# Gate and up projections by one level of Strassen's algorithm, in two passes over the weights

## The chip, the cores and the metric

The kernel runs on one core of one Trainium2 chip. Its time is the device time of one execution in microseconds (us); of before there are three runs. Times inside an execution are read from one profiled execution by the hardware profiler. TensorE (PE) multiplies matrices, VectorE (DVE), ScalarE (ACT) and GpSimd (POOL) work on vectors, and SyncE (SP) issues the DMA transfers, in the order of its own queue.

## The reference

One layer of a conditioned hybrid decoder, on a sequence of 2048 rows with a model width of 1024 and a feed-forward width of 2816:

```python
h   = _modulate(x, ln1_g[l], sh1, sc1)         # RMSNorm, scale and shift
u   = h @ w_in[l]                              # queries, keys, values of both head groups
...                                            # fox attention (8 heads x 64), differential attention (4 x 128)
x = x + g1[:, None, :] * (mixed @ w_out[l])
h2 = _modulate(x, ln2_g[l], sh2, sc2)
y = (jax.nn.silu(h2 @ w_gate[l]) * (h2 @ w_up[l])) @ w_down[l]
x = x + g2[:, None, :] * y
```

Inputs and output are f32. The change touches the last four lines.

## The kernel before

**Precision.** Every large product is made from 16-bit floats. An f32 operand is scaled by a power of two, cast to fp16 (the high part, on ScalarE, `cast_scaled`, L139) and the rest is cast again (the low part, on VectorE, `sub_scaled`, L144). A product is then three matmuls: high x high, high x low, low x high. The scale comes from a bound: the largest absolute value of each row (`absmax`, VectorE, L123), then the largest of the column of 128 (`colmax`): by GpSimd's all-reduce over partitions (L104), or, if a bank's tag is given, by a matmul that transposes the column into a bank of PSUM (L108) and a VectorE maximum (L109). `pow2` (L115 to L119) makes the scale in four small VectorE operations.

**Stages.** The attention of eight head groups runs first, and ends near 1600 us. The out projection (`out_proj`) makes the new `x` in 16 blocks of 128 rows; a block's row statistics follow at once. All 16 blocks of the new `x` stay on chip (`x1s`), in tiles of four. `norm2` normalises a block, splits it into high and low, and transposes it by a DMA (L953) into `h2s`. Blocks 0 to 7 are done beside attention and out projection, blocks 8 to 15 inside the first chunk below.

**Feed-forward.** 2816 columns are 22 tiles of 128. The loop at the end of `trunk` runs over 11 chunks `c` of two tiles, and in each over four groups `tck` of 512 rows. For a group, `gate_up` makes four results of 128x512 (two tiles, gate and up), each by 8 x 3 matmuls (L1036) in a bank of tags `st` or `pv`; `swiglu` joins gate and up (L1042 on ScalarE, L1043 on VectorE). One step later the joined tile is bounded (`act_row`), split (`act_split`) and multiplied by the down weight: `down` has 16 blocks of 128x512 a chunk and four rows each, six matmuls to a block (L1068), and VectorE adds each bank onto the rows of `x1s` (L1070). So the down products of a group lie between the gate/up products of the next one. Each weight is loaded once: `gu_load` (L981), `gu_row`, `gu_scale`, `gu_split` for gate and up, `dn_load` (L1006; VectorE's bound L1007, GpSimd's product with the gate row L1008), `dn_row`, `dn_scale`, `dn_split` for down. `weight_steps` says at which of 16 steps of a chunk the next chunk's weights are treated.

**What sets the order.** The code is written in the order of these loops; the framework then reorders the instructions of each engine by its own model of their times (`schedule_with_timeline_sim=True`). The order on an engine is fixed in the program, and an instruction that waits holds back those behind it on its engine. Buffers come from pools: `stage()` has three buffers of 128x1024 f32, the large tiles `htile()` and `mtile()` four each of 128x4096 f32, and PSUM has banks of the tags `ip` (1), `st` (2), `pv` (2) and `mx` (3).

## Time and profile before

| | us |
|---|---|
| median of 3 runs | 3000.74 |
| the runs | 2998.21 to 3001.41 |
| the profiled execution | 3000.15 |
| its span in the trace | 2998.4 |
| TensorE busy, of the span | 2819.1 |
| VectorE busy | 1816.3 |
| ScalarE busy | 1199.1 |
| GpSimd busy | 1016.1 |

The profiled execution's time is 1.75 us above its span. The mean granted clock of TensorE over the span is 0.986 of full speed. In a row of the trace, L1036 is line 1036 of the kernel, `out<-in` are the tiles that an instruction writes and reads, and what stands in brackets is the idle time of the engine just before, and what ended it. Matmuls overlap one another, so their single durations (some 0.38 us) add up to more than the time they take together; what one costs is the length of a stretch over their number.

### The profile page before, as it was taken

To read this page: it belongs to the slowest core of one execution; us is meant where nothing else is said; L and a number is where in the kernel's file an instruction comes from. 1 tells how busy PE (TensorE), PEld (TensorE's weight loads), DVE (VectorE), ACT (ScalarE), POOL (GpSimd) and SP (SyncE) were. 2 spreads that over 40 slices of the span, in tenths; PEclk is the share of its full clock that TensorE was granted. 3 is DMA by queue.
4 is the path that set the end of the run, shared out by engine and by line. 5 is a ranking of instruction groups with operands and counts; after the bars stand their busy time and mean duration, and the time that the engine had idled before them with its cause. 6 is when DMAs were issued, how large, how long until landed. Compare 5 with 4: busy or idle time off the path is not lost.

```text
span 2998.4 us, 49306 instructions
## 1 busy us (share of the span) xinstructions
PE 2819.1 (94%) x19346; PEld 1524.8 (51%) x19346; DVE 1816.3 (61%) x3883; ACT 1199.1 (40%) x2323; POOL 1016.1 (34%) x1073
## 2 busy tenths in 40 slices
...
GB/s 225 78 77 59 61 75 38 81 48 65 71 53 90 51 96 101 61 124 107 131 104 105 93 27 29 21 22 35 22 29 22 29 28 22 29 22 31 12 22 91
DMA packets 227530, 186.40 MB, mean 62 GB/s; under 512 B 176984, under 2 KB 193752, under 8 KB 227040
## 3 DMA queue, kind: packets, MB, share of 16 engines
...
q14 instruction: 83, 0.68, 0.1%
...
## 4 chain that ended last, share of the span: by engine, by line
PE 52%; DVE 4%; DMA 3%; ACT 2%; POOL 1%; issue 1%; SPq 0%; POOLq 0%; ACTq 0%; DVEq 0%
PE ps_mx L1068 14%; PE ps_pv L1036 14%; PE ps_st L1036 14%; PE ps_ip L929 3%; PE ps_ip L437 2%; DMA wide<-wide 1%; PE ps_mx L546 1%; PE ps_st L579 1%; PE ps_st L580 1%; DVE stg L952 0%; PE ps_pv L609 0%; POOL pxs L593 0%; DMA stg<-in_w_down_dram 0%; DMA mt<-stg 0%; ACT pxs L585 0%
## 5 line engine op out<-in xcount | busy, mean ns | idle before, releaser
L593 POOL TENSOR_TENSOR pxs<-pxs 128x512 f16<-128x512 f32 (+3 forms) x640 | 693.6, 1099 | 383.7 <-ACT pxs L590 214.2
L437 PE MATMUL ps_ip<-wbuf,ht 128*128 128x384 f16 (+1 forms) x2952 | 569.4, 335 | 20.4 <-DVE vts L144 9.1
L1068 PE MATMUL ps_mx<-dnb,wide 128*128 128x512 f16 x2112 | 485.5, 380 | 13.4 <-DVE ht L1070 10.5
L585 ACT ACTIVATE pxs<-ps_st,cells 128x512 f32<-128x512 f32 (+3 forms) x640 | 390.7, 620 | 251.5 <-PE ps_st L580 117.0
L437 PEld LDWEIGHTS <-ht 128*128 128x128 f16 x3072 | 298.8, 100 | 259.8 <-issue 69.8
L1036 PEld LDWEIGHTS <-mt 128*128 128x128 f16 x2688 | 263.0, 98 | 320.4 <-ACT mt L139 3.5
L104 POOL PARTITION_ALL_REDUCE t_cm<-t_am x84 | 32.7, 398 | 1060.4 <-DVE t_am L123 1037.2
L1070 DVE SCALAR_TENSOR_TENSOR ht<-ps_mx,t_ai,ht 128x512 f32<-128x512 f32 x264 | 196.6, 747 | 302.5 <-PE ps_mx L1068 302.5
L590 ACT ACTIVATE pxs<-pxs 128x512 f16<-128x512 f32 (+3 forms) x640 | 351.2, 565 | 10.5
L607 PE MATMUL ps_pv<-vts,pxs 128*128 128x129 f16 (+1 forms) x2176 | 341.6, 206 | 5.2 <-DVE os L626 5.0
L608 PE MATMUL ps_pv<-vts,pxs 128*128 128x128 f16 (+1 forms) x2176 | 343.8, 208 | 0.0
L609 PE MATMUL ps_pv<-vts,pxs 128*128 128x129 f16 (+1 forms) x2176 | 326.5, 206 | 18.0 <-POOL pxs L593 17.4
L1068 PEld LDWEIGHTS <-wide 128*128 128x128 f16 x2112 | 206.6, 98 | 264.1 <-issue 11.9
L548 DVE TENSOR_REDUCE t_mxc<-ps_mx 128x1 f32<-128x512 f32 x384 | 256.1, 681 | 68.3 <-PE ps_mx L546 67.3
L139 ACT ACTIVATE wide<-wide,t_as 128x1024 f16<-128x1024 f32 x44 | 50.5, 1148 | 597.5 <-DVE t_as L116 597.5
L1036 PEld LDWEIGHTS <-gub 128*128 128x128 f16 x1536 | 150.7, 98 | 185.0 <-issue 3.2
L546 PE MATMUL ps_mx<-mt 71*128 71x512 f16 (+7 forms) x640 | 198.9, 350 | 47.6 <-DVE t_mxc L548 37.7
L609 PEld LDWEIGHTS <-pxs 128*128 128x128 f16 x2176 | 206.7, 98 | 64.0 <-POOL pxs L593 32.4
L607 PEld LDWEIGHTS <-pxs 128*128 128x128 f16 x2176 | 207.5, 97 | 54.1 <-ACT pxs L585 3.5
L1042 ACT ACTIVATE wide<-ps_st,t_gi 128x512 f32<-128x512 f32 x88 | 60.2, 684 | 432.1 <-PE ps_st L1036 432.0
L579 PE MATMUL ps_st<-mt 67*128 67x512 f16 (+7 forms) x640 | 223.7, 350 | 6.6 <-ACT pxs L585 6.3
L608 PEld LDWEIGHTS <-pxs 128*128 128x128 f16 x2176 | 207.4, 97 | 37.7 <-issue 7.3
...
## 6 DMA issues: line engine op xcount, KB each, us to landing
...
```

Of the source, the lines that this page charges most:

```text
L437: T.matmul(pt[:, 0:N], lhsT=h4[:, k, hs, c : c + P], rhs=w4[k // 4][:, k % 4, ws, 0:N], start=(i == 0), stop=(i == len(terms) - 1))
L546: T.matmul(b[:, 0:w], lhsT=QA[0:K, qb * P : (qb + 1) * P], rhs=K2[0:K, c0 : c0 + w], start=True, stop=True)
L548: V.tensor_reduce(out=mx[:, 4 * j + n : 4 * j + n + 1], in_=b[:, 0:w], op=ALU.max, axis=AX.X)
L579: T.matmul(b[:, c0:QC], lhsT=K2[0:K, kb * P : (kb + 1) * P], rhs=QA[0:K, q0:q1], start=True, stop=False, skip_group_check=True)
L585: A.activation(p32[:, c0:QC], b[:, c0:QC], AF.Exp, bias=pshift, scale=1.0)
L590: A.activation(ph[:, c0:QC], p32[:, c0:QC], AF.Copy, bias=0.0, scale=1.0)
L593: (V if hilo[1] == "V" else G).tensor_tensor(out=pl[:, c0:QC], in0=p32[:, c0:QC], in1=ph[:, c0:QC], op=ALU.subtract)
L607: T.matmul(pv[:, jj, :], lhsT=lhs_h, rhs=v4[:, kb, h, 0 : W + 1], start=first, stop=False, skip_group_check=True)
L608: T.matmul(pv[:, jj, 0:W], lhsT=lhs_h, rhs=v4[:, kb, h, W + 2 : 2 * W + 2], start=False, stop=False, skip_group_check=True)
L609: T.matmul(pv[:, jj, :], lhsT=lhs_l, rhs=v4[:, kb, h, 0 : W + 1], start=False, stop=end, skip_group_check=True)
L1036: T.matmul(b.rearrange("p (b n) -> p b n", b=4), lhsT=e["g"][:, w, k, ws, :], rhs=h4[:, :, 2 * k + hs, :], start=(k == 0 and z == 0), stop ...
L1068: T.matmul(b, lhsT=aT[:, as_, f, j * P : (j + 1) * P], rhs=dn[f][:, ws, n * 512 : (n + 1) * 512], start=(f == 0 and z == 0), stop=(f == CH ...
```

## The change

Gate and up are computed by one level of Strassen's algorithm. A pair of tiles (256 columns), a sum over 1024 and a half of the rows are each cut in two, so that a result of four quarters of 128x512 takes seven products of half the depth in place of eight. There are now two passes over the rows (the even and odd blocks of 1024 rows are the two halves of a product's columns), each over all 11 pairs of tiles; a step `q` of the new loop is one pair in one pass, 22 in all, and `w` is 0 for gate and 1 for up. Gate, up and down weights are loaded and split in each pass, so twice.

- Each product (`product`) has 4 x 3 matmuls, and the products run in the order 4, 5, 1, 2, 3, 7, 6. Products 2 and 3 are added onto the banks of 4 and 5, after ScalarE has copied these. The other sums of the quarters are made by VectorE from PSUM and by GpSimd between tiles on chip; then Silu and the product of gate and up.
- Five sums of the weights are made by GpSimd (`gu_sum`) from a raw tile of 128x2048, of which there is one (`raw`); the host packs gate and up weights so that a load is 1 MB. The bound is taken over 2048 columns, with a factor of two.
- Seven sums of the normalised rows are needed (`norm_sum`): two blocks are normalised (`norm_row`), added or subtracted on GpSimd, split, and transposed by a DMA. For the first half they go to four tiles on chip (`comb`) beside attention and out projection; for the second half they are made in the steps q = 2, 4, 6, 8, stored to DRAM (`hcd`), and loaded onto the first half's in step 10.
- The new `x` is stored to DRAM (`x1d`) by `out_proj`; eight blocks are loaded back for the first pass, and the other eight when the first are done, in step 11. `out_proj` has two buffers of two blocks.
- All column maxima of this part are made by the matmul on the bank `ip`; before, only the first chunk's were. The activation is bounded and split once a step, 128x2048 (`act_scale`, `act_split`), in one buffer, and the down products of a step lie in slots 4 to 13 of the next one (`DOWNAT`).

The diff, with the lines it removes shown only where the code printed above isn't enough:

```diff
+        if blk == 0:
+            hs.extend(htile() for _ in range(4))
+        x1 = pairbuf(blk // 2)[:, blk % 2, :]
...
+            x = x1[:, n * 512 : (n + 1) * 512]
+            V.scalar_tensor_tensor(out=x, in0=b, scalar=do, in1=x, op0=ALU.mult, op1=ALU.add)
+        nc.sync.dma_start(x1d[blk], x1)
...
+    ORDER = (4, 5, 1, 2, 3, 7, 6)
+    BSUM = {1: ((0, 0), ALU.add, (1, 1)), 2: ((0, 0), None, None), 3: ((1, 0), ALU.subtract, (1, 1)), 4: ((0, 1), ALU.subtract, (0, 0)), 5: ((1, 1), None, None), 6: ((0, 0), ALU.add, (1, 0)), 7: ((0, 1), ALU.add, (1, 1))}
+    ASUM = ((1, 1, ALU.add, 2), (2, 3, ALU.add, 2), (5, 1, ALU.add, 0), (6, 3, ALU.subtract, 1), (7, 0, ALU.subtract, 2))
+    APOS = {3: 0, 4: 1, 1: 2, 2: 3, 5: 4, 6: 5, 7: 6}
...
+    def comb(i):
+        c = ORDER.index(i)
+        return hs[c // 2][:, (c % 2) * 2048 : (c % 2 + 1) * 2048].bitcast(F16).rearrange("p (b k n) -> p b k n", b=4, n=P)
...
+    def norm_row(jj, z):
+        if jj < 4:
+        y = ys[jj][z]
+        blk = 2 * jj + z
+        V.scalar_tensor_tensor(out=y, in0=y, scalar=r2[:, blk : blk + 1], in1=mod[:, 0:D], op0=ALU.mult, op1=ALU.mult)
+        V.tensor_tensor(out=y, in0=y, in1=mod[:, D:], op=ALU.add)
+    def norm_sum(jj, i):
+        (za, ha), op, other = BSUM[i]
+        e = stage()
+        src = ys[jj][za][:, ha * 512 : (ha + 1) * 512]
+        if other:
+            zb, h = other
+            G.tensor_tensor(out=e[:, 0:512], in0=src, in1=ys[jj][zb][:, h * 512 : (h + 1) * 512], op=op)
+            src = e[:, 0:512]
+        hl = e[:, 512:1024].bitcast(F16).rearrange("p (k s n) -> p k s n", k=4, s=2)
+        s3 = src.rearrange("p (k n) -> p k n", k=4)
+        A.activation(hl[:, :, 0, :], s3, AF.Copy, bias=0.0, scale=1.0)
+        V.tensor_tensor(out=hl[:, :, 1, :], in0=s3, in1=hl[:, :, 0, :], op=ALU.subtract)
+        row = hl.rearrange("p k s n -> p (k s n)")
+        if jj < 4:
+            nc.sync.dma_start(comb(i)[:, jj], row, transpose=True)
+        else:
+            tr = e[:, 0:512].bitcast(F16)
+            nc.sync.dma_start(tr.rearrange("p (k n) -> p k n", n=P), row, transpose=True)
+            nc.sync.dma_start(hcd[ORDER.index(i), jj - 4], tr)
...
+    uhm = w1.tile([P, 2048], F32, tag="UH", bufs=1, name="uhm")
+    run(flat(last[TAIL : ends[1]]), outs[0:3])
+    run(flat(last[ends[1] : ends[2]]), outs[3:4] + norm_pair(0) + outs[4:6])
+    run(flat(last[ends[2] :]), norm_pair(1) + outs[6:8] + norm_pair(2) + outs[8:10] + norm_pair(3))
...
+    def gu_load(q, w):
+        nc.sync.dma_start(raw, t["w_gu"][q % NPAIR, w])
+    def gu_bound(q, w):
+        sets[q]["am", w] = absmax(raw, BF16)
+    def gu_sum(k):
+        _, a, op, b = ASUM[k]
+        G.tensor_tensor(out=sums[:, k * 512 : (k + 1) * 512], in0=raw[:, a * 512 : (a + 1) * 512], in1=raw[:, b * 512 : (b + 1) * 512], op=op)
...
+    def gu_split(q, w, part):
+        src, c0, c1 = ((raw[:, 512:1536], 0, 8), (sums[:, 0:1536], 8, 20), (sums[:, 1536:2560], 20, 28))[part]
+        src = src.rearrange("p (c n) -> p c n", n=P)
+        s = sets[q]["s", w]
+        cast_scaled("A", aw[w][:, c0:c1, 0, :], src, s)
+        sub_scaled(aw[w][:, c0:c1, 1, :], src, s, aw[w][:, c0:c1, 0, :])
...
+    def product(q, w, i):
+        e = sets[q]
+        tgt = {2: 4, 3: 5}.get(i, i)
+        fresh = tgt == i
+        if fresh:
+            e["b", w, i] = bank(k0[i])
+        b = e["b", w, tgt]
+        cb = comb(i)
+        for k in range(4):
+            for z, (ws, hb) in enumerate(((0, 0), (0, 1), (1, 0))):
+                T.matmul(b.rearrange("p (b n) -> p b n", b=4), lhsT=aw[w][:, APOS[i] * 4 + k, ws, :], rhs=cb[:, :, 2 * k + hb, :], start=(fresh and k == 0 and z == 0), stop=(k == 3 and z == 2), skip_group_check=True)
+        gi = e["gi", w]
+        if i == 4:
+            A.activation(s4s, b, AF.Copy, bias=0.0, scale=1.0)
+        elif i == 5:
+            A.activation(s5s, b, AF.Copy, bias=0.0, scale=1.0)
+            G.tensor_tensor(out=s4s, in0=s4s, in1=s5s, op=ALU.subtract)
+        elif i == 1:
+            V.tensor_tensor(out=tmp, in0=b, in1=s4s, op=ALU.add)
+        elif i == 2:
+            A.activation(dif, b, AF.Copy, bias=0.0, scale=1.0)
+            if w == 0:
+                A.activation(act[:, 0, 1], b, AF.Silu, bias=0.0, scale=gi)
+            else:
+                V.tensor_tensor(out=act[:, 0, 1], in0=b, in1=act[:, 0, 1], op=ALU.mult)
+        elif i == 3:
+            V.tensor_tensor(out=dif, in0=b, in1=dif, op=ALU.subtract)
+            if w == 0:
+                A.activation(act[:, 1, 0], b, AF.Silu, bias=0.0, scale=gi)
+            else:
+                V.tensor_tensor(out=act[:, 1, 0], in0=b, in1=act[:, 1, 0], op=ALU.mult)
+        elif i == 7:
+            if w == 0:
+                V.tensor_tensor(out=act[:, 0, 0], in0=b, in1=tmp, op=ALU.add)
+                A.activation(act[:, 0, 0], act[:, 0, 0], AF.Silu, bias=0.0, scale=gi)
+            else:
+                V.tensor_tensor(out=s5s, in0=b, in1=tmp, op=ALU.add)
+                G.tensor_tensor(out=act[:, 0, 0], in0=s5s, in1=act[:, 0, 0], op=ALU.mult)
+        else:
+            V.tensor_tensor(out=tmp, in0=b, in1=tmp, op=ALU.add)
+            if w == 0:
+                G.tensor_tensor(out=act[:, 1, 1], in0=tmp, in1=dif, op=ALU.add)
+                A.activation(act[:, 1, 1], act[:, 1, 1], AF.Silu, bias=0.0, scale=gi)
+            else:
+                G.tensor_tensor(out=tmp, in0=tmp, in1=dif, op=ALU.add)
+                G.tensor_tensor(out=act[:, 1, 1], in0=tmp, in1=act[:, 1, 1], op=ALU.mult)
+    def act_scale(q):
+        e = sets[q]
+        g = colmax(absmax(uhm, BF16), "ip")
...
+    def down(q, th, j, n):
+        b = bank("mx")
+        for f in range(2):
+            for z, (as_, ws) in enumerate(((0, 0), (0, 1), (1, 0))):
+                T.matmul(b, lhsT=aT[:, th, as_, f, j * P : (j + 1) * P], rhs=dnb[:, (2 * q + f) % 4, ws, n * 512 : (n + 1) * 512], start=(f == 0 and z == 0), stop=(f == 1 and z == 2))
+        r = 2 * j + th
+        xb = x1s[r // 4][:, r % 4, :]
+        xs = xb[:, n * 512 : (n + 1) * 512]
+        V.scalar_tensor_tensor(out=xs, in0=b, scalar=sets[q]["ai"], in1=xs, op0=ALU.mult, op1=ALU.add)
...
+    def up_head(q):
+        return [(0, gu_load, q, 1), (1, gu_bound, q, 1)] + [(1 + k // 2, gu_sum, k) for k in range(5)] + [(2, gu_scale, q, 1)]
+    def up_tail(q):
+        return [(0, gu_split, q, 1, 0), (1, gu_split, q, 1, 1), (2, gu_split, q, 1, 2)]
+    downs = [(th, j, n) for th in range(2) for j in range(4) for n in range(2)]
+    DOWNAT = (0, 0, 0, 0, 2, 2, 2, 2, 2, 2, 1, 1, 1, 1)
+    NQP = 2 * NPAIR
+    for q in range(NQP + 1):
+        st = [[] for _ in range(14)]
+        if q < NQP:
+            for k, f, *a in up_tail(q):
+                at(k, f, *a)
+            for f in range(2):
+                at(3 + f, dn_load, q, f)
+            at(5, dn_scale, q)
+            for f in range(2):
+                at(9 + f, dn_split, q, f)
+        if q:
+            at(0, act_scale, q - 1)
+            at(1, act_split, q - 1, 0)
+            at(2, act_split, q - 1, 1)
+        if q + 1 < NQP:
+            at(2, gu_load, q + 1, 0)
+            at(3, gu_bound, q + 1, 0)
+            for k in range(5):
+                at(3 + k // 2, gu_sum, k)
+            at(4, gu_scale, q + 1, 0)
+            for k in range(3):
+                at(7 + (k + 1) // 2, gu_split, q + 1, 0, k)
+            for k, f, *a in up_head(q + 1):
+                at(9 + k, f, *a)
+        if q in (2, 4, 6, 8):
+            jj = 4 + q // 2 - 1
+            for z in range(2):
+                at(8, norm_load, jj, z)
+                at(9 + z, norm_row, jj, z)
+            for k, i in enumerate(ORDER):
+                at(min(13, 10 + k // 2), norm_sum, jj, i)
+        nd = 0
+        for slot in range(14):
+            w, i = slot // 7, ORDER[slot % 7]
+            if q < NQP:
+                product(q, w, i)
+                if q == NPAIR - 1 and w == 1:
+                    c = ORDER.index(i)
+                    nc.sync.dma_start(comb(i).rearrange("p b k n -> p b (k n)"), hcd[c].rearrange("b p n -> p b n"))
+            if q:
+                for _ in range(DOWNAT[slot]):
+                    down(q - 1, *downs[nd])
+                    nd += 1
+            for f in st[slot]:
                 f()
-            if late and q == 3:
```

On VectorE, a steady step: before, a chunk's maximum over the activation (`t_am<-wide`), its small operations and the split stand between evictions of the down products (L1070).

```order
L1043 SCALAR_TENSOR_TENSOR wide<-ps_pv,t_gi,wide 128x512 [waits PE_49,Activation_49]
L123 TENSOR_REDUCE t_am<-wide 128x1 [waits DVE_49]
L1070 SCALAR_TENSOR_TENSOR mt<-ps_mx,t_ai,mt 128x512 [waits PE_49]
L115 TENSOR_SCALAR t_p2a<-t_cm 128x1 [waits Pool_49]
L1070 SCALAR_TENSOR_TENSOR mt<-ps_mx,t_ai,mt 128x512 [waits PE_49]
L116 TENSOR_SCALAR t_as<-t_p2a 128x1 [waits DVE_49]
```

After, in the last step's turn to the next, L1120 reads the last product of `up`, L123 on `uhm` is the activation's maximum, L123 on `vts` the next raw weight's, L1099 reads the next step's product 1, L109 is the column maximum that closes the bound, L1153 is an eviction of a down product.

```order
L1120 TENSOR_TENSOR pxm<-ps_mx,pxm 128x512 [waits DVE_49,PE_49]
L144 SCALAR_TENSOR_TENSOR mt<-pxm,t_ws,mt 128x8x128 [waits Activation_49]
L1153 SCALAR_TENSOR_TENSOR mt<-ps_mx,t_ai,mt 128x512 [waits PE_49]
L123 TENSOR_REDUCE t_amh<-uhm 128x1 [waits Pool_49]
L123 TENSOR_REDUCE t_amh<-vts 128x1 [waits DMAHW2_49]
L1099 TENSOR_TENSOR pxm<-ps_st,mt 128x512 [waits PE_49,Pool_49]
L109 TENSOR_REDUCE t_cm<-ps_ip 128x1 [waits PE_49]
```

The maximum now waits for GpSimd, and the reads of the next step's products stand behind it.

On GpSimd, after, at the same turn: L1038 is a weight sum, L1125 adds to the last product's sum, L1126 multiplies it by the gate's, L1097 belongs to the next product 5.

```order
L1062 TENSOR_TENSOR stg<-stg,grep_22080 128x1024 [waits DMAHW5_49,DVE_49]
L1118 TENSOR_TENSOR uhm<-mt,uhm 128x512 [waits DVE_49]
L1038 TENSOR_TENSOR pxm<-vts 128x512 [waits DMAHW6_49,Activation_49,Pool_49]
L1038 TENSOR_TENSOR pxm<-vts 128x512 [waits Pool_49] x2
L1125 TENSOR_TENSOR pxm<-pxm,wide 128x512 [waits DVE_49]
L1038 TENSOR_TENSOR pxm<-vts 128x512 [waits DVE_49]
L1038 TENSOR_TENSOR pxm<-vts 128x512 [waits Pool_49]
L1126 TENSOR_TENSOR uhm<-pxm,uhm 128x512 [waits Pool_49]
L1097 TENSOR_TENSOR mt<-mt 128x512 [waits Activation_49]
```

Here two weight sums stand between the two last operations on the activation; before, GpSimd had in this stretch only its product with the gate row (L1008) and the all-reduce (L104).

On SP, after, in a step that also normalises: L1031 loads a raw weight, L967 a row block, L995 transposes a summed row and L996 stores it.

```order
L967 DMA stg<-x1d 128x1024 [waits DMAHW1_49,DVE_49]
L995 DMA_TRANSPOSE stg<-stg 128x8x128 [waits DMAHW2_49,DVE_49]
L996 DMA hcd<-stg 128x1024 [waits DMAHW2_49]
L995 DMA_TRANSPOSE stg<-stg 128x8x128 [waits DMAHW3_49,DVE_49]
L996 DMA hcd<-stg 128x1024 [waits DMAHW5_49,DMAHW4_49]
L1031 DMA vts<-in_w_gu_dram 128x2048 [waits DMAHW0_49,DMAHW6_49,DVE_49,Pool_49]
L995 DMA_TRANSPOSE stg<-stg 128x8x128 [waits DMAHW5_49,DVE_49]
```

A raw weight's load stands behind transposes and stores that wait for VectorE and for one another; before, SP had only weight loads in this part, and the output's stores at the end.

## Rows read from the trace of the kernel before

**Rows 1.** The page, section 1: busy time, share of the span, instructions.

```profile
PE 2819.1 (94%) x19346; PEld 1524.8 (51%) x19346; DVE 1816.3 (61%) x3883; ACT 1199.1 (40%) x2323; POOL 1016.1 (34%) x1073
```

**Rows 2.** The page, section 4: the chain that ended last, by line.

```profile
PE ps_mx L1068 14%; PE ps_pv L1036 14%; PE ps_st L1036 14%; PE ps_ip L929 3%; PE ps_ip L437 2%; DMA wide<-wide 1%; PE ps_mx L546 1%; PE ps_st L579 1%; PE ps_st L580 1%; DVE stg L952 0%; PE ps_pv L609 0%; POOL pxs L593 0%; DMA stg<-in_w_down_dram 0%; DMA mt<-stg 0%; ACT pxs L585 0%
```

**Rows 3.** Windows by stage: length, busy us (instructions) by engine, clock, DMA share, GB/s.

```profile
core 0: us, PE busy (x) PEld busy (x) DVE busy (x) ACT busy (x) POOL busy (x), PEclk, DMA share, GB/s
1366.00:1612.00 246.00, 233.50 (x1697) 117.97 (x1696) 139.60 (x241) 131.56 (x230) 80.75 (x70) 1.00 0.49 118
1612.00:1750.00 138.00, 119.66 (x539) 52.94 (x537) 93.74 (x158) 34.17 (x37) 14.53 (x14) 0.95 0.27 72
1750.00:2978.00 1228.00, 1228.00 (x5692) 556.71 (x5690) 543.35 (x1003) 158.22 (x172) 71.95 (x101) 1.00 0.09 26
...
1580.00:1600.00 20.00, 19.43 (x90) 8.59 (x89) 11.97 (x19) 10.41 (x15) 0.00 (x0) 1.00 0.87 197
```

**Rows 4.** TensorE in order of time, the end: start, length, line, tiles, count.

```profile
2978.60 15.94 PE L1068 MATMUL ps_mx<-dnb,wide 128*128 128x512 f16 x72
```

**Rows 5.** TensorE in order of time, 1613 to 1715 us.

```profile
1613.35 0.22 PE L108 MATMUL ps_ip<-idb,t_amh 128*128 128x128 bf16 x1
1613.40 1.24 PE L1036 MATMUL ps_pv<-ht,gub 128*128 128x512 f16 x5
...
1617.88 1.03 PE L1036 MATMUL ps_st<-ht,mt 128*128 128x512 f16 x2 [3.18 <-ACT mt L139]
...
1650.04 1.47 PE L1068 MATMUL ps_mx<-dnb,wide 128*128 128x512 f16 x6 [2.38 <-ACT wide L139]
...
1659.54 2.33 PE L1036 MATMUL ps_st<-h2n,gub 128*128 128x512 f16 x10 [1.82 <-DMA h2n<-stg]
...
1709.76 2.72 PE L1068 MATMUL ps_mx<-dnb,wide 128*128 128x512 f16 x6 [10.55 <-DVE ht L1070]
1712.27 2.58 PE L1036 MATMUL ps_st<-mt,gub 128*128 128x512 f16 x9
```

**Rows 6.** VectorE by line, 1612 to 2998 us: count, busy us, mean ns, idle before.

```profile
L1070 DVE SCALAR_TENSOR_TENSOR ht<-ps_mx,t_ai,ht 128x512 f32<-128x512 f32 x264 | 196.6, 747 | 302.5 <-PE ps_mx L1068 302.5
...
L123 DVE TENSOR_REDUCE t_am<-wide 128x1 f32<-128x1024 f32 x44 | 53.7, 1220 | 1.4
...
L144 DVE SCALAR_TENSOR_TENSOR mt<-stg,t_ws,mt 128x1024 f16<-128x1024 f32 x28 | 35.9, 1280 | 10.2 <-ACT mt L139 10.1
...
L118 DVE TENSOR_SCALAR t_p2b<-t_p2a 128x1 f32<-128x1 f32 x97 | 13.6, 144 | 0.0
...
L948 DVE TENSOR_TENSOR stg<-stg,mt 128x1024 f32<-128x1024 f32 x8 | 11.8, 1474 | 0.0
```

**Rows 7.** GpSimd by line, whole span.

```profile
L593 POOL TENSOR_TENSOR pxs<-pxs 128x512 f16<-128x512 f32 x448 | 553.0, 1247 | 297.8 <-ACT pxs L590 185.0 <-issue 56.6 <-PE ps_pv L609 15.1
...
L1008 POOL TENSOR_TENSOR stg<-stg,grep 128x1024 f32<-128x1024 f32 x22 | 52.7, 2395 | 269.8 <-DVE t_dam L1007 262.6 <-DVE mt L144 7.2
```

**Rows 8.** ScalarE by line, 1550 to 2998 us.

```profile
L1042 ACT ACTIVATE wide<-ps_st,t_gi 128x512 f32<-128x512 f32 x88 | 60.2, 684 | 432.1 <-PE ps_st L1036 432.0
L139 ACT ACTIVATE wide<-wide,t_as 128x1024 f16<-128x1024 f32 x44 | 50.5, 1148 | 597.5 <-DVE t_as L116 597.5
```

**Rows 9.** VectorE and GpSimd in order of time, near 1625 us.

```profile
1624.06 1.28 DVE L947 SCALAR_TENSOR_TENSOR stg<-ht,cells,mt 128x1024 f32<-128x1024 f32 x1
1625.37 3.26 DVE L948 TENSOR_TENSOR stg<-stg,mt 128x1024 f32<-128x1024 f32 x1
1624.28 3.27 POOL L1008 TENSOR_TENSOR stg<-stg,grep 128x1024 f32<-128x1024 f32 x1 [19.28 <-DVE t_dam L1007]
```

**Rows 10.** DMA issues on SP and their readers, in order of time.

```profile
1994.45 0.33 SPq L1006 DMA_DIRECT2D stg<-in_w_down_dram  x1
1997.80 1.22 DVE L1007 TENSOR_REDUCE t_dam<-stg 128x1 f32<-128x1024 f32 x1 [2.71 <-DMA stg<-in_w_down_dram]
1561.64 1.77 SPq L923 DMA_TRANSPOSE wide<-wide  x1
1566.15 1.15 ACT L139 ACTIVATE wide<-stg,cells 128x1024 f16<-128x1024 f32 x1 [3.50 <-DMA wide<-wide]
```

More of the change, by code (lines that the diff above doesn't have):

```diff
@@ L958, in trunk, with norm_pair @@
+    def norm_pair(jj):
+        return [(0.2, lambda z=z: norm_row(jj, z)) for z in range(2)] + [(0.2, lambda i=i: norm_sum(jj, i)) for i in ORDER]
     ends = []
@@ new lines, in trunk @@
+    pxm = w1.tile([P, 3072], F32, tag="PX", bufs=1, name="pxm")
+    sums, tmp = pxm[:, 0:2560], pxm[:, 2560:3072]
+    raw = vts[:, 1].rearrange("p b n -> p (b n)")[:, 0:4096].bitcast(F32)
+    dnb = wide[:, 0:4096].bitcast(F16).rearrange("p (a s n) -> p a s n", a=4, s=2)
+    dif = wide[:, 4096:4608]
+    act = uhm.rearrange("p (t f n) -> p t f n", t=2, f=2)
+    sets = [{} for _ in range(2 * NPAIR)]
+    def gu_load(q, w):
+        nc.sync.dma_start(raw, t["w_gu"][q % NPAIR, w])
+    def gu_bound(q, w):
+        sets[q]["am", w] = absmax(raw, BF16)
@@ L1030, in gate_up @@
-    def gate_up(c, f, tck, w):
-        e = sets[c]["gu"][f]
-        h4 = h2view(tck)
-        b = bank("st" if w == 0 else "pv")
-        for k in range(KT):
-            for z, (ws, hs) in enumerate(((0, 0), (0, 1), (1, 0))):
-                T.matmul(b.rearrange("p (b n) -> p b n", b=4), lhsT=e["g"][:, w, k, ws, :], rhs=h4[:, :, 2 * k + hs, :], start=(k == 0 and z == 0), stop=(k == KT - 1 and z == 2))
-        return b
-    def swiglu(c, f, bs):
-        gi = sets[c]["gu"][f]["gi"]
-        a32 = act[:, 0].rearrange("p (f n) -> p f n", f=CH)
-        A.activation(sls[:, f], bs[0], AF.Silu, bias=0.0, scale=gi[:, 0:1])
-        V.scalar_tensor_tensor(out=a32[:, f, :], in0=bs[1], scalar=gi[:, 1:2], in1=sls[:, f], op0=ALU.mult, op1=ALU.mult)
@@ L1077, in first_weights @@
-    def first_weights():
-        for w in range(2):
-            gu_load(0, 0, w)
-            gu_row(0, 0, w)
-            gu_scale(0, 0, w)
-            gu_split(0, 0, w)
-    run(flat(last[TAIL : ends[1]]), outs[0 : OUTSPLIT[0]])
-    run(flat(last[ends[1] : ends[2]]), outs[OUTSPLIT[0] : OUTSPLIT[1]])
-    h2s.append(htile())
-    early = [(1, lambda blk=blk: norm2(blk)) for blk in range(4)] + [(1, first_weights)]
-    run(flat(last[ends[2] :]), outs[OUTSPLIT[1] : OUTSPLIT[2]], early)
-    run(outs[OUTSPLIT[2] : 13])
@@ new lines, in trunk, with act_split @@
+    aT = hs[3][:, 2048:4096].bitcast(F16).rearrange("p (t s f n) -> p t s f n", t=2, s=2, f=2)
+    def act_scale(q):
+        e = sets[q]
+        g = colmax(absmax(uhm, BF16), "ip")
+        e["as"] = small(1, "as", bufs=3)
+        e["ai"] = small(1, "ai", bufs=3)
+        pow2(g, e["as"], e["ai"])
+        V.tensor_scalar(out=e["ai"], in0=e["ai"], scalar1=e["di"], scalar2=e["gi", 1], op0=ALU.mult, op1=ALU.mult)
+    def act_split(q, th):
+        s = sets[q]["as"]
+        src = act[:, th].rearrange("p f n -> p (f n)")
+        hi, lo = (aT[:, th, z].rearrange("p f n -> p (f n)") for z in range(2))
+        cast_scaled("A", hi, src, s)
+        sub_scaled(lo, src, s, hi)
```

249 lines of the change are left out of this document (74 added, 175 removed).

## The prediction

> **What bounds the kernel now.** I read the page first: TensorE is busy 94% of the span, VectorE 61%, ScalarE and GpSimd less [rows 1], and in the chain that ended last TensorE holds the largest share, with the matmuls of the gate/up and the down projections as its costliest lines [rows 2]. Then the windows by stage, since the change touches only the end of the out projection and the feed-forward part. From 1750 to 2978 us TensorE is busy 1228.00 of 1228.00 us: 5692 matmuls, so 215.7 ns each, at granted clock 1.00, with VectorE busy 543.35 us, 44% [rows 3]. In that stretch nothing but the number of matmuls counts. Before it, 1612 to 1750 us, the same work starts up with gaps and a clock of 0.95; before that (1366 to 1612 us) attention and the out projection overlap, with DMA at 0.49, and 0.87 between 1580 and 1600 us [rows 3]. The last 72 matmuls of the down projection run alone at the end [rows 4].
>
> The sum starts from the profiled execution, 3000.15 us, which is the median of the runs, 3000.74 us, within 0.02%. A measurement of this kernel can tell about 0.2%, 6 us, from no change.
>
> **1. Matmuls.** Gate and up: 22 tiles x 2 weights x 4 row groups x 24 = 4224 matmuls of 128x512 become 22 passes x 2 weights x 7 products x 12 = 3696. The down projection keeps 2112 (22 x 16 x 6). So 528 fewer x 215.7 ns = **-113.8 us**; both forms read a moving operand of 512 columns in four blocks, so I take the same 215.7 ns. Everything else is what eats into this.
>
> **2. More bounds on TensorE.** Each pass now has four column maxima done by a transposing matmul (two weights, the down weight, the activation): 84 more than before. One is 0.22 us, and the next matmul starts 0.05 us after it [rows 5]. So 4 to 18 us; I take 0.1 each, **+8**.
>
> **3. Start.** The gaps at 1617.88, 1650.04, 1659.54 and 1709.76 us are 3.18, 2.38, 1.82 and 10.55 us, 17.9 together, and after the last the clock was low: 6 matmuls took 2.72 us where 6 take 1.47, and 9 took 2.58 [rows 5]. The 10.55 us gap is a wait for VectorE, which had normalised blocks 8 to 15 between the evictions; that work is now elsewhere. I take -20. The new kernel has its own start (two weights of 1 MB with five sums, bounds and casts before the first products of `up`, one raw buffer): 0 to 20, taken +10. **-10** together.
>
> **4. The steady passes.** One pass is 168 + 96 = 264 matmuls, 56.9 us. What the other engines have to do in it, by durations:
> VectorE: three maxima over 2048 columns at twice 1.22 (7.3), two over 1024 (2.4), subtractions of the splits: 2 x (1024 + 1536 + 1024) for the weights, 2 x 1024 for the activation, 2 x 1024 for the down weight, at 1.28 per 1024 (9.0 + 2.6 + 2.6), ten reads of products and sixteen evictions at 0.75 (19.5), some 20 small ones at 0.14 (2.9): 46.3 us, 81% of the pass [rows 6]. Before it was 44%.
> GpSimd: ten sums of 128x512 of the weights and six of the combination at 1.25, two products with the gate row at 2.40: 24.8 us [rows 7]. ScalarE: casts at 1.15 per 1024 (8.0 + 4.6) and ten reads of 512 at 0.68: 19.4 us [rows 8].
> So no engine's sum reaches 56.9. But there is less room, and two things use it. The first is contention: at 1625.37 us a VectorE addition with two SBUF operands lasted 3.26 us beside a GpSimd product that lasted 3.27 [rows 9], where the other seven of that line average (8 x 1.474 - 3.26)/7 = 1.22 [rows 6] and the GpSimd line averages 2.40 [rows 7]. Ten subtractions of that kind stand in a pass (14 us), and GpSimd is busy 44% of the time; when they meet the loser waits for about half a GpSimd operation, 0.6 us: 10 x 0.44 x 0.6 = 2.7 us on VectorE, between 0 (they never meet) and 16 x 1.25 = 20 (every GpSimd sum blocks one).
>
> The Trainium skill says in "SBUF — State Buffer", section "Who interferes with whom", that VectorE's second port pair is GpSimd's own and is locked for a whole instruction. It speaks against this change, which puts sums on GpSimd beside subtractions on VectorE; the 3.26 us beside 1.22 agree with it. By the rule alone the 2.7 us would be a lower end for what the two engines cost each other, since GpSimd too is held up.
>
> The second is the chain from the last product to the first down matmul of a pass, with its activation tile kept only once: VectorE reads product 6 (0.75), GpSimd adds and multiplies (2 x 1.25; in every second pass two weight sums stand between these two in its queue, 2.5), VectorE's maximum (2.4), the matmul for the column maximum (0.22), six small operations (0.9), cast (1.15), subtraction (1.28): 9.2 or 11.7 us, with queueing behind evictions up to 15. In TensorE's new order 74 to 85 matmuls stand between product 6 and the first down product, 16.0 to 18.3 us, and the matmul of the column maximum stands after 46 to 64 of these, 9.9 to 13.8 us, with 6.1 to 8.6 us of the chain ahead of it. So it just fits; in VectorE's queue the maximum waits for GpSimd, and behind it stand the next weight's maximum and the reads of the next products, which TensorE needs for its banks. I take 1.5 us of waits a pass x 21 = **+31.5**; the lower end is 0, the upper the whole chain without cover, 9.2 x 21 = 193.
>
> **5. Four passes that also normalise.** In passes 2, 4, 6 and 8 VectorE gets two rows x two operations at 1.28 and 1.22 (5.0) and seven subtractions of 512 columns (4.5): 56 us of a pass, as much as TensorE's. Each summed row goes through one free stage buffer: GpSimd 1.25, ScalarE and VectorE 0.6 each, then a transposing DMA and a store. A 512 KB weight took 3.35 us from issue to its reader (1994.45 to 1997.80), a transpose of 512 KB 4.5 (1561.64 to 1566.15) [rows 10]; half of each is 2.2 and 1.7, so 6.4 us at least and 10.3 at most, times seven, 45 to 72 us of SP's in-order queue, in which the weights of the next pass stand behind. 0 to 15 a pass, taken 4 x 4 = **+16**.
>
> **6. The middle.** Between the halves 7 MB of summed rows come back and 8 rows are stored and reloaded (8 MB), all on SP beside the weights. At the 197 GB/s of 1580 to 1600 us [rows 3] that is 15 / 0.197 = 76 us of transfer within two passes (114 us). 0 to 25, taken **+8**.
>
> **7. The end.** The last pass has nothing to cover its activation chain: 9.2 us less what stands before, then 96 matmuls with the clock low at first, as after the gap of 10.55. Before, the chain was covered by a gate/up product and 72 matmuls ran alone [rows 4]. **+10** (5 to 14).
>
> **8. The out projection.** Near its end DMA was the busiest resource (0.87 at 1580 to 1600 us) [rows 3], and it now has sixteen rows stored and eight reloaded (12 MB, 61 us at 197 GB/s), and 28 half transposes in place of 8 whole ones. Most of it lies earlier, under attention, where the share was 0.49. **+12** (-5 to 40).
>
> Sum: 3000.15 - 113.8 + 8 - 10 + 31.5 + 16 + 8 + 10 + 12 = 2962; I say **2960 us**.
>
> **The rivals.**
> *The whole gain.* The scheduler finds cover for the chain and for the normalising passes: terms 4 and 5 go to about nothing, 2915 us. For it: no engine's sum reaches a pass. Against: 81% and single buffers.
> *VectorE and GpSimd set the pass: slower.* Without term 4 the sum is 2931, so 69 us of waits bring it back: 3.3 us in each of 21 passes decide. The place is VectorE's queue between product 6 and the activation split: the maximum over 2048 columns waits for GpSimd, which waits behind its weight sums, and TensorE then waits at the column maximum, at each first down product, or for a bank. With 5.7 us a pass it is 2931 + 120 = 3050 us. For it: 46.3 us plus up to 20 of contention is more than 56.9. Against: 12 of the 46.3 us are evictions with a bank to spare, and one operation in eight met its rival in the rows of before.
> *DMA bounds the out projection and the middle.* Terms 6 and 8 at their upper ends, 45 us more: 3005 us at most, 2990 with part of it hidden. For it: 0.87 in the rows; against: that was 20 us only.
>
> **Chances.** The forecast 0.50 (its own range 2930 to 2992), the whole gain 0.14, VectorE and GpSimd 0.24, DMA 0.12. The range 2910 to 3035 leaves out a small part of the whole gain (0.05) and the upper half of the second rival (0.13). Faster by over 0.2%: 0.48 + 0.14 + half of the DMA case (0.06), 0.68; slower 0.24; within 0.2% 0.08.
>
> **What will show it.** Right: 264 matmuls plus four short ones a pass at 215.7 ns, TensorE's idle time in a steady pass between 0.5 and 3 us, put down to VectorE or ScalarE at the column maximum or the first down product; VectorE about 80% busy; the normalising passes longer by 2 to 8 us. The whole gain: passes of 57 to 58 us throughout. The second rival: passes over 60 us with VectorE over 90% busy, subtractions well over 1.28 us per 1024. The third: gaps on DMA before 1620 us and around pass 10. Wrong altogether: a matmul that is no longer 215.7 ns, or a clock under 1.00 in the steady passes.

## The result and the profile after

The changed kernel takes 2961.81 us (median of 4 runs, 2959.26 to 2965.83) where the kernel before takes 3001.07 beside it: a ratio of 0.987, 95% interval 0.9853 to 0.9888. 2960 was predicted. The profiled execution has a span of 2962.2 us, 36.2 less than before. As shown below, this sum came out right with three of its terms wrong.

The page, section 1, answers to [rows 1]:

```profile
PE 2726.8 (92%) x18902; PEld 1478.2 (50%) x18902; DVE 2212.0 (75%) x4205; ACT 1410.4 (48%) x2597; POOL 1590.5 (54%) x1392
```

TensorE has 444 matmuls fewer, VectorE and GpSimd have taken on 396 and 574 us. To see where TensorE waits, the windows by stage, as in [rows 3]. The bounds are the out projection's last matmul (1623 us) and the starts of the first, the eleventh and the last activation maximum (L123 on `uhm`), of which there is one a pass:

```profile
core 0: us, PE busy (x) PEld busy (x) DVE busy (x) ACT busy (x) POOL busy (x), PEclk, DMA share, GB/s
1500.00:1623.00 123.00, 114.95 (x668) 54.26 (x667) 57.37 (x89) 44.20 (x83) 46.44 (x35) 0.96 0.72 206
1623.00:1669.00 46.00, 42.57 (x192) 18.73 (x191) 31.47 (x53) 26.86 (x31) 24.92 (x18) 0.96 0.29 103
1669.00:2302.00 633.00, 581.30 (x2640) 257.95 (x2639) 502.65 (x708) 191.38 (x228) 328.65 (x205) 0.98 0.30 93
2302.00:2931.50 629.50, 624.06 (x2921) 284.01 (x2919) 475.44 (x703) 188.71 (x213) 269.96 (x182) 1.00 0.18 62
2931.50:2962.00 30.50, 22.52 (x97) 9.77 (x97) 17.87 (x25) 2.19 (x2) 0.00 (x1) 0.89 0.35 138
```

The ten passes of the third window take 63.3 us each, the eleven of the fourth 57.2. 264 matmuls at the 215.7 ns of [rows 3] are 56.9 us, so the later passes stand at the floor of TensorE's work, with VectorE busy 76% and GpSimd 43%, and the loss of 61 us lies in the first ten. For 51.7 us of these ten (633.00 less 581.30) TensorE is idle; the rest is mostly the lower clock, 0.98 on average against 1.00. GpSimd has 33 us a pass there in place of 25, VectorE 50 in place of 43. The later passes alternate between some 54 and 61 us from maximum to maximum, so only their sum counts; TensorE waits 3.3 us in them, in one pass after the reload of `x`.

What TensorE waits for from 1560 us on: us in total, times, the longest:

```profile
PE ps_ip L108 <- DVE t_amh L123: 26.7, 9, 8.1
PE ps_mx L1149 <- DVE mt L1153: 12.1, 9, 2.8
PE ps_mx L1149 <- ACT ht L139: 10.0, 7, 3.4
PE ps_st L1091 <- DVE pxm L1099: 3.5, 8, 1.3
```

The largest is the one foreseen in the second rival: the matmul of the activation's column maximum. The longest case of it, in order of time, on GpSimd, then VectorE, then TensorE:

```profile
1982.24 2.24 POOL L1125 TENSOR_TENSOR pxm<-pxm,wide 128x512 f32<-128x512 f32 x1 [5.94 <-DVE pxm L1120]
1984.45 1.26 POOL L1097 TENSOR_TENSOR mt<-mt 128x512 f32<-128x512 f32 x1
1985.68 6.14 POOL L1038 TENSOR_TENSOR pxm<-vts 128x512 f32<-128x512 f32 x5
1991.78 1.25 POOL L1126 TENSOR_TENSOR uhm<-pxm,uhm 128x512 f32<-128x512 f32 x1
...
1993.07 2.29 DVE L123 TENSOR_REDUCE t_amh<-uhm 128x1 bf16<-128x2048 f32 x1 [7.23 <-POOL uhm L1126]
...
1995.41 0.29 PE L108 MATMUL ps_ip<-idb,t_amh 128*128 128x128 bf16 x1 [8.11 <-DVE t_amh L123]
1996.01 4.85 PE L1091 MATMUL ps_st<-ht,mt 128*128 128x512 f16 x12 [0.31 <-DVE pxm L1099]
```

Five weight sums, 6.14 us, stand between the two operations that finish the activation. The next twelve matmuls took 4.85 us where twelve take 2.75: TensorE had stood idle from 1987.3 us, and the granted clock was 0.50, the lower of its two levels (1.2 GHz), from 1990.0 to 2000.2 us and 1.00 (2.4 GHz) behind it. In the later passes at most two weight sums stand there, and the chain is covered. But this is the one case with five: of the first ten passes one more has two weight sums in that place, and eight have none. So the weight sums explain this wait and not the 61 us.

The end, which answers to [rows 4]:

```profile
2933.88 0.29 PE L108 MATMUL ps_ip<-idb,t_amh 128*128 128x128 bf16 x1 [4.50 <-DVE t_amh L123]
2936.17 22.23 PE L1149 MATMUL ps_mx<-wide,ht 128*128 128x512 f16 x96 [2.00 <-ACT ht L139]
```

The 96 matmuls at the end take 1.4 us more than at 215.7 ns each: the granted clock was 0.50, the lower level, from 2932.1 to 2938.9 us; it fell within the wait of 4.50 us.

And a column maximum among matmuls in a later pass, as in [rows 5]; the next one starts 0.06 us after it:

```profile
2883.78 0.22 PE L108 MATMUL ps_ip<-idb,t_amh 128*128 128x128 bf16 x1
2883.84 4.05 PE L1091 MATMUL ps_pv<-ht,mt 128*128 128x512 f16 x18
```

Contention is there also in the passes without waits. By line, 2425.7 to 2828.5 us, VectorE and then GpSimd:

```profile
L144 DVE SCALAR_TENSOR_TENSOR wide<-stg,t_dws,wide 128x1024 f16<-128x1024 f32 x14 | 25.2, 1837 | 3.9 <-ACT wide L139 3.9
...
L144 DVE SCALAR_TENSOR_TENSOR mt<-vts,t_ws,mt 128x1024 f16<-128x1024 f32 x14 | 17.9, 1281 | 3.7 <-ACT mt L139 3.2
...
L1122 POOL TENSOR_TENSOR uhm<-pxm,wide 128x512 f32<-128x512 f32 x7 | 15.3, 2182 | 17.6 <-DVE pxm L1120 17.6
...
L1125 POOL TENSOR_TENSOR pxm<-pxm,wide 128x512 f32<-128x512 f32 x7 | 8.9, 1265 | 8.3 <-DVE pxm L1120 8.3
```

The first row's mean, 1.84 us, mixes two cases: ten of its 14 subtractions overlap an operation of GpSimd and take 1.87 to 2.29 us, four do not and take 1.27; none of the second row's overlaps one, and they take 1.28. Of the two additions on GpSimd, that of L1122 begins beside a running subtraction in every pass and takes 2.18, that of L1125 is alone or the first to begin and takes 1.27. One case of each, in order of time:

```profile
2447.41 1.27 DVE L144 SCALAR_TENSOR_TENSOR mt<-pxm,t_ws,mt 128x1024 f16<-128x1024 f32 x1
2447.63 2.19 POOL L1122 TENSOR_TENSOR uhm<-pxm,wide 128x512 f32<-128x512 f32 x1 [3.02 <-DVE pxm L1120]
...
2530.96 1.27 POOL L1125 TENSOR_TENSOR pxm<-pxm,wide 128x512 f32<-128x512 f32 x1 [2.77 <-DVE pxm L1120]
2531.22 2.09 DVE L144 SCALAR_TENSOR_TENSOR mt<-pxm,t_ws,mt 128x1024 f16<-128x1024 f32 x1 [0.34 <-ACT mt L139]
2532.30 2.14 POOL L1126 TENSOR_TENSOR uhm<-pxm,uhm 128x512 f32<-128x512 f32 x1
```

That is what the Trainium skill says in "SBUF — State Buffer", section "Who interferes with whom": the one that comes second waits until the other is done, and either engine can be the one.

### The profile page after: what moved, and what is told of

The parts are those of the page before. It is cut to its first block, busy times and chain, and to the rows that moved or that the text cites. A ratio compares the mean times of both kernels' runs of the same rounds, so it can differ in the third digit from the quotient of the medians.

```text
span 2962.2 us, 49590 instructions
## 1 busy us (share of the span) xinstructions
PE 2726.8 (92%) x18902; PEld 1478.2 (50%) x18902; DVE 2212.0 (75%) x4205; ACT 1410.4 (48%) x2597; POOL 1590.5 (54%) x1392
## 5 line engine op out<-in xcount | busy, mean ns | idle before, releaser
L593 POOL TENSOR_TENSOR pxs<-pxs 128x512 f16<-128x512 f32 (+3 forms) x640 | 686.7, 1088 | 344.9 <-ACT pxs L590 180.7
L1091 PEld LDWEIGHTS <-mt 128*128 128x128 f16 x3696 | 361.1, 98 | 445.8 <-issue 18.4
L1149 PE MATMUL ps_mx<-wide,ht 128*128 128x512 f16 x2112 | 505.1, 382 | 24.2 <-DVE mt L1153 12.1
L1038 POOL TENSOR_TENSOR pxm<-vts 128x512 f32<-128x512 f32 x220 | 296.8, 1376 | 335.2 <-DMA vts<-in_w_gu_dram 308.2
L437 PEld LDWEIGHTS <-ht 128*128 128x128 f16 x3072 | 296.7, 100 | 254.9 <-issue 61.4
L1091 PE MATMUL ps_st<-ht,mt 128*128 128x512 f16 x1584 | 382.1, 384 | 8.4 <-DVE pxm L1099 3.5
L1091 PE MATMUL ps_pv<-ht,mt 128*128 128x512 f16 x1584 | 379.1, 379 | 0.0
L1149 PEld LDWEIGHTS <-ht 128*128 128x128 f16 x2112 | 206.5, 99 | 281.1 <-issue 27.9
L1153 DVE SCALAR_TENSOR_TENSOR mt<-ps_mx,t_ai,mt 128x512 f32<-128x512 f32 x352 | 256.3, 742 | 65.4 <-PE ps_mx L1149 65.0
L580 PE MATMUL ps_st<-mt 128*128 128x512 f16 (+3 forms) x640 | 223.4, 349 | 0.0
```

The source lines that it names most:

```text
L437: T.matmul(pt[:, 0:N], lhsT=h4[:, k, hs, c : c + P], rhs=w4[k // 4][:, k % 4, ws, 0:N], start=(i == 0), stop=(i == len(terms) - 1))
L593: (V if hilo[1] == "V" else G).tensor_tensor(out=pl[:, c0:QC], in0=p32[:, c0:QC], in1=ph[:, c0:QC], op=ALU.subtract)
L1038: G.tensor_tensor(out=sums[:, k * 512 : (k + 1) * 512], in0=raw[:, a * 512 : (a + 1) * 512], in1=raw[:, b * 512 : (b + 1) * 512], op=op)
L1091: T.matmul(b.rearrange("p (b n) -> p b n", b=4), lhsT=aw[w][:, APOS[i] * 4 + k, ws, :], rhs=cb[:, :, 2 * k + hb, :], start=(fresh and k == ...
L1149: T.matmul(b, lhsT=aT[:, th, as_, f, j * P : (j + 1) * P], rhs=dnb[:, (2 * q + f) % 4, ws, n * 512 : (n + 1) * 512], start=(f == 0 and z = ...
L1153: V.scalar_tensor_tensor(out=xs, in0=b, scalar=sets[q]["ai"], in1=xs, op0=ALU.mult, op1=ALU.add)
```

## The experiments

The theory after the result: the waits of passes 1 to 10 come from the normalising and summing of the second half's rows, which is spread over these passes, and the products of the change cost nothing beside TensorE's time. The rival: the first half waits by itself. All kernels start from the changed one. Medians of 4 runs, ratios to the kernel before on the same chip; the last two columns are from one profiled execution each, in us from maximum to maximum (from the first to the eleventh, and from there to the last).

| kernel | us | ratio (95%) | first ten passes | last eleven |
|---|---|---|---|---|
| the change | 2961.81 | 0.987 (0.9853 to 0.9888) | 633 | 630 |
| e1 no normalising | 2907.19 | 0.9691 (0.9668 to 0.9714) | 576 | 628 |
| e2 sum before product 6 | 2957.86 | 0.9867 (0.9847 to 0.9887) | 621 | 632 |
| e3 later down products | 2954.56 | 0.9846 (0.983 to 0.9862) | 624 | 625 |
| e4 neither transposes nor stores | 2923.86 | 0.975 (0.9731 to 0.9769) | 595 | 633 |
| e7 stores on ScalarE's queue | 2969.85 | 0.99 (0.9886 to 0.9915) | 637 | 628 |
| e8 rows normalised early | 2945.65 | 0.9823 (0.9804 to 0.9842) | 611 | 629 |
| e9 and their own buffers | 2932.98 | 0.9777 (0.9761 to 0.9793) | 600 | 630 |
| e10 e9 with e2 and e3 | 2943.62 | 0.9812 (0.9797 to 0.9826) | 605 | 635 |
| e11 weight sums twice | 3035.39 | 1.0113 (1.0094 to 1.0133) | 653 | 669 |
| e12 no transposes | 2958.9 | 0.9853 (0.9839 to 0.9868) | 618 | 633 |
| e13 no stores | 2960.53 | 0.9855 (0.9835 to 0.9875) | 619 | 633 |
| e14 e9 with e2 | 2936.82 | 0.978 (0.9766 to 0.9795) | 600 | 632 |

**Is it the normalising work?** e1 takes it out (`if False:` for `if q in (2, 4, 6, 8):`, and no reload from `hcd`).

> Left out: the normalising and summing of the second half's rows in passes 2, 4, 6 and 8 and their reload in pass 10 (the second pass multiplies the first half's sums again). Theory N: the waits of passes 1 to 10 (a pass of 63.6 us where the later ones take 57.5) are all caused by this normalising work; without it passes 1 to 10 also take 57 to 58.5 us, and the time is 2962 - 10 x 6 = about 2900 us (2893 to 2910). Rival P: the first half waits by itself (its chain of product 6, GpSimd, maximum, split does not fit yet, or its buffers are late from the start), and the later passes only run well because they have settled; then passes 1 to 10 stay over 61 us and the time is over 2940 us.

Passes 1 to 10 fell to 57.6 us each, 57 us in all, and the whole time by 55. The windows of e1, first ten and last eleven passes:

```profile
1669.80:2245.50 575.70, 569.41 (x2657) 258.15 (x2656) 457.45 (x664) 178.03 (x199) 285.24 (x187) 1.00 0.17 57
2245.50:2873.00 627.50, 621.55 (x2904) 282.17 (x2902) 475.24 (x704) 188.28 (x212) 266.24 (x180) 1.00 0.19 62
```

The theory holds, the rival falls: all but 4 us of the 61 go with the normalising work, and TensorE's idle time in these passes falls from 51.7 to 6.3 us.

**Is it GpSimd's place in the chain?** e2 and e3 shorten or cover the chain:

```diff
 # e2, after product 3; product 6 then adds only its bank to dif
+            G.tensor_tensor(out=dif, in0=dif, in1=tmp, op=ALU.add)
 # e3 (act_scale and act_split one slot later too)
-    DOWNAT = (0, 0, 0, 0, 2, 2, 2, 2, 2, 2, 1, 1, 1, 1)
+    DOWNAT = (0, 0, 0, 0, 0, 2, 2, 2, 2, 2, 2, 2, 1, 1)
```

> GpSimd adds the difference and the running sum (dif + tmp) right after product 3 instead of after product 6, so that one GpSimd operation (1.27 us, 2.25 when it meets a subtraction) and the weight sums queued between it and the next one leave the chain from product 6 to the activation's maximum. Nothing is left out. If GpSimd's place in this chain makes the waits of the first half (TensorE at L108 for the maximum, 26.7 us, and at L1149 for the cast, 10.0 us), these fall to under 10 us together and the time is 2935 to 2945 us. If VectorE's load or late transfers make them, the time stays within 8 us of 2962.

> The bound, the splits and the first down products of a pass are written one slot (12 matmuls, 2.6 us) later; nothing is left out. If the waits are a chain that comes a little too late, each of the some 10 waits of the first half gets 2.6 us more cover and the time falls by 15 to 25 us, to 2937 to 2947 us. If the waits come from VectorE or GpSimd being behind in all, the wait moves with the work and the time stays within 6 us of 2962, or is longer, since the activation's buffer is then held longer against the next pass's product 2.

The intervals of both overlap with the change's own: 4 and 7 us of the whole time that can't be told from nothing. TensorE's waits at L108 were still 20.1 and 26.1 us, and the first ten passes took 12 and 9 us less, of 61. So GpSimd's place in the chain has a share at most; most of the delay has another source.

**Vector work or transfers?** e4 leaves out the transposes (L995), stores (L996) and reload; e12 only the transposes, e13 only stores and reload; e7 has `nc.scalar.dma_start` for the store.

> Left out: the transposes of the second half's summed rows, their stores and their reload; loads of x, normalising, sums and splits on VectorE, GpSimd and ScalarE stay. Theory N in two forms: if the serial transposes and stores on SP, with the weights' loads behind them, are the cause, this behaves as the kernel without normalising, 2895 to 2910 us. If the vector work is the cause (some 68 us of VectorE in the first half, and GpSimd's sums in its queue), the waits stay and the time is 2945 to 2960 us.

> The 28 stores of the second half's summed rows are issued by ScalarE's queue in place of SP's; nothing is left out. Leaving out transposes and stores gave 38 of the 55 us that the normalising work costs. Form Q: SP's in-order queue is the cause, since each store there waits some 3 us for its transpose while weights' loads stand behind; then half of the 38 us goes, 2938 to 2950 us. Form B: the three stage buffers are the cause (two hold the normalised rows, one is left for the sums and the down weights, held until the store has ended); then the time stays within 6 us of 2962, or is longer by what ScalarE now waits.

> Left out: the transposes of the second half's summed rows; the split rows are stored as they are and reloaded. If the transposes (1.25 us of SP's issue each, some 3 us to landing) make the 38 us of transposes and stores, the time is 2925 to 2935 us; if the stores make it, within 8 us of 2962.

> Left out: the stores of the second half's summed rows and their reload; the transposes stay. If the transposes make the 38 us, within 10 us of 2962; if the stores do (another DMA's time in which the stage buffer is held), 2925 to 2940 us. If both this and the last kernel gain about half, it is the time that a buffer is held, whichever DMA holds it.

e4 gains 38 us of the 55 and lies between its two forms, so the smaller part is vector work. For SP's queue e7 gives no sign: with the stores on the other queue 8 us were lost (the two intervals just touch), with TensorE's waits at L108 at 42.9 us; the transposes stayed on SP's queue, so it is not tested whole. e12 and e13 gained 3 and 1 us in all, each as the form has it by which the other transfer makes the 38 us, and both can't be so. The profiled executions tell more. In the first ten passes the two gained 15 and 14 us against 38 together; TensorE's idle time there, 51.7 us in the change, is 38.3 in e12, 35.4 in e13 and 23.4 in e4, so the two gains, 13 and 16 us, add up to about the 28 of both. So in the passes each transfer costs about the same, as the third reading of e13 has it. The whole time hides it, since the first maximum came 8 and 10 us later than in the change and the last eleven passes gave back 3. Up to some 1760 us all engines of these kernels have the same instructions in the same order as in the change, so the later first maximum is not the edit's doing; what makes it stays open.

**The buffers.** e8 normalises the second half's rows in the out projection and stores them a second time; e9 also puts them where scale and shift stood, which frees two of the three stage buffers.

```diff
+    def row_early(blk):                      # e8: after the out projection of the block
+        y = pairbuf(blk // 2)[:, blk % 2, :]
+        V.scalar_tensor_tensor(out=y, in0=y, scalar=r2[:, blk : blk + 1], in1=mod[:, 0:D], op0=ALU.mult, op1=ALU.mult)
+        V.tensor_tensor(out=y, in0=y, in1=mod[:, D:], op=ALU.add)
+        nc.sync.dma_start(yd[blk - 8], y)
-        ys[jj][z] = stage()                  # e9
+        ys[jj][z] = mod[:, z * D : (z + 1) * D]
```

> The rows of the second half are normalised in the out projection, in place after their store, and stored a second time (4 MB); the passes load them normalised, into the stage buffers as before. So the passes lose 16 VectorE operations of 128x1024 (30 us with the contention of the trace) but keep all sums, transposes and stores. Form B or Q: the time falls by the vector part alone, 17 us at most, less up to 8 us that the out projection gets longer: 2945 to 2960 us.

> As the kernel with rows normalised early, and the two loaded row blocks now stand in the 8 KB that held scale and shift, which nobody needs any more, instead of in two of the three stage buffers. Form B (stage buffers): sums and down weights have all three buffers, and most of the 38 us goes: 2915 to 2930 us. Form Q (SP's queue): the same transposes and stores stand in the same queue, and the time is that of the kernel before this one, within 8 us: 2940 to 2960 us.

e8 gained 16 us, e9 13 more. That is between the two forms of e9: the buffers have a part, but not most of the 38 us. How a buffer that is still held reaches TensorE can be seen in the change itself. In its first ten passes GpSimd waits for stores to `hcd` before a sum of rows (L984), and VectorE, before the subtraction of such a sum (L989), for the cast that stands behind GpSimd's sum (us in total, times, the longest):

```profile
POOL stg L984 <- DMA hcd<-stg: 67.6, 11, 10.7
DVE stg L989 <- ACT stg L988: 50.8, 18, 5.3
```

An operation of the activation can stand behind that wait, as in the second longest wait of TensorE at L108:

```profile
1789.88 1.27 POOL L984 TENSOR_TENSOR stg<-stg 128x512 f32<-128x512 f32 x1 [4.80 <-DMA hcd<-stg]
1791.11 1.27 POOL L1125 TENSOR_TENSOR pxm<-pxm,wide 128x512 f32<-128x512 f32 x1
...
1798.87 0.29 PE L108 MATMUL ps_ip<-idb,t_amh 128*128 128x128 bf16 x1 [4.97 <-DVE t_amh L123]
```

The sum that L1125 adds to was there at 1784.6 us, and GpSimd was free at 1785.1. With the transposes left out (e12) GpSimd's waits for stores fall to 21.0 us.

e9 computes everything and beats both kernels, at 0.9777 of the one before. Its windows:

```profile
1675.50:2276.00 600.50, 572.53 (x2633) 256.60 (x2634) 476.65 (x692) 192.78 (x227) 315.25 (x204) 0.99 0.31 97
2276.20:2905.90 629.70, 624.15 (x2922) 283.69 (x2920) 475.76 (x704) 188.75 (x213) 269.76 (x183) 1.00 0.18 62
```

> As the last one, with the sum before product 6 and the down products one slot later, which gave 4 and 7 us alone. Nothing is left out. If what is left of the waits is the chain from product 6 to the first down product, the time is 2900 to 2920 us; if the two edits only moved waits that the buffers made, it is that of the last kernel within 5 us.

> Rows normalised early, their buffers in the old place of scale and shift, and the sum before product 6; the down products stay where they were. Nothing is left out. The kernel with later downs as well lost 8 us in the pass in which the rows of x are stored and reloaded; if that was the later downs' doing, this one has 2918 to 2930 us, else it is at 2935 to 2945.

With the small edits of e2 and e3 on top it is 11 us slower, with that of e2 alone not to be told from e9 (0.978 to 0.9777). The later down products are the difference between e10 and e14 (0.9812 against 0.978, with intervals just apart): 4 us of it lie in the first ten passes and 4 in one pass after them, of 65.1 us in e10 and 61.5 in e14, where the others of either kernel have 57.2. SP's queue and VectorE in that pass of e10, in order of time:

```profile
2332.73 0.42 SPq L1170 DMA_DIRECT2D out_dram<-mt  x1
2337.81 0.32 SPq L1172 DMA_DIRECT2D mt<-x1d  x1
2338.23 0.38 SPq L1041 DMA_DIRECT2D vts<-in_w_gu_dram  x1
...
2344.74 2.29 DVE L123 TENSOR_REDUCE t_amh<-vts 128x1 bf16<-128x2048 f32 x1 [6.53 <-DMA vts<-in_w_gu_dram]
```

A raw weight's load stands behind reloads of `x`, each of which waits up to 4.9 us for the store of finished rows before it. VectorE waits 6.53 us for the load, then 4.85 us for GpSimd, which makes the five sums of that weight first, and the operations that scale the activation stand behind both; TensorE waits 5.7 us in that pass. It is the third rival's place, at a small price; e14 has 3.8 us of waits there and the changed kernel 3.3.

**How much room was there?** e11 makes each weight sum twice.

```diff
+        for _ in range(2):
+            G.tensor_tensor(out=sums[:, k * 512 : (k + 1) * 512], ...
```

> Each of the ten weight sums of a pass is made twice by GpSimd (the second writes the same values): 12.5 us more of GpSimd a pass and more contention for VectorE. If the steady pass has room on both engines (the later passes of the changed kernel show no wait at all, VectorE 78% and GpSimd 47% busy), passes 12 to 21 stay at 57.5 us and the loss falls on passes 1 to 10, 1 to 3 us each: 2970 to 2995 us. If GpSimd's place in the chain from product 6 to the split is all that stands between the change and its slower rival, every pass loses at least 2.5 to 5 us (two more sums between the last two operations, and contention): 3015 us and more.

The whole gain is gone, and it is 31 us slower than the kernel before, which took 3004.21 beside it. TensorE's waits from 1560 us on and the windows of e11:

```profile
PE ps_ip L108 <- DVE t_amh L123: 51.1, 17, 12.9
PE ps_st L1092 <- DVE pxm L1100: 25.5, 18, 3.1
PE ps_mx L1150 <- DVE mt L1154: 17.5, 26, 3.0
...
1677.30:2330.00 652.70, 594.55 (x2664) 262.06 (x2665) 512.40 (x704) 194.16 (x228) 473.74 (x306) 0.96 0.29 89
2330.00:2999.00 669.00, 633.39 (x2892) 282.58 (x2889) 485.07 (x703) 186.55 (x211) 418.46 (x279) 0.98 0.18 58
```

The later passes, which had hardly a wait, now take 60.8 us, 3.6 more, with GpSimd busy 63% and VectorE 73%: neither is full, and yet TensorE waits. The first ten passes take 2.0 us more each. My first expectation, that the steady passes had room, is refuted. The run does not part the two ways in which the added sums can cost, by their place in the chain and by the contention they bring.

## Why the prediction was right

Term by term against the profiled executions:

- *Matmuls, -113.8:* right (528 x 215.7 ns are 113.9). The later passes stand at 264 x 215.7 ns and four column maxima of 0.06 us. So *more bounds on TensorE* are 5 us, not 8.
- *Start, -10:* about -4. Before lost 24 us between the out projection's end (1611.8 us) and its last matmul against 215.7 ns a matmul; after loses 20 in the same part, with passes and end taken out.
- *The steady passes, +31.5:* wrong, about 4. With the normalising taken out (e1) the passes take 57.6 and 57.1 us on average. VectorE's and GpSimd's sums were near (43 and 25 us a pass against 46.3 and 24.8), the contention is there (1.87 to 2.29 us against 1.28), and the cover in TensorE's order was enough for all of it. (The part of the chain ahead of the column maximum adds up to 5.7 or 8.2 us by its own terms, not 6.1 or 8.6; that changes nothing here.)
- *Four passes that also normalise, +16:* mis-sized; this is the step that failed. It measured 57 us. I had taken 4 us in each of four passes; it is some 6 a pass over nine, since the scheduler spread the work over passes 1 to 9 (the tenth has none of it and no wait). The term had the sums' serial path as time of SP's queue. What the runs show is that 38 of the 55 us go with the two transfers, in about equal parts, and that buffers of their own give 13 back; a held buffer stops GpSimd and VectorE, as in the wait at 1798.87 us. That all of the 38 us arise in this way is not shown.
- *The middle, +8:* about nothing: TensorE waits 3.3 us in the last eleven passes, which hold it, and these take 629.5 us where 11 passes of 56.9 us with their bounds are 629. In e10 a pass there took 8 us more.
- *The end, +10:* about 8, waits of 4.50 and 2.00 us and 1.4 us at the lower clock.
- *The out projection, +12:* its last matmul ends at 1622.9 us against 1611.8, 11.1 later with 13 more gate/up matmuls done by then, so about 8. Kernels with the same code there ended it between 1619.4 and 1632.5 us, so this term is not known to better than that.

So 31.5 + 16 + 8 = 55.5 stood for 61: the place was wrong and the sum right by luck. By its own signs the steady passes were those of the first rival, 57 us each, and the first ten those of the second, 63.3 us, though with VectorE busy 79% and not over 90%.

The second rival was right in the place of the largest wait, TensorE at the column maximum behind VectorE and GpSimd. Its price was not: 3.3 us of waits in each of 21 passes, 69 us in all, were to turn the gain into a loss. The change loses 61 us in its passes, 2.9 a pass, and is still 39 us faster; e11 loses 120, 5.7 a pass, and is 31 us slower. The turning point lies between. But 12.5 us more of GpSimd's work a pass were enough to reach the other side, with no vector engine over 80%.
